# RMSNorm with swish on one core: the first 32 rows stored through GpSimd's queue, in two pieces

## The chip, the cores and the metric

The kernel runs on one core of a Trainium2 chip. The core has five engines with instruction streams of their own: TensorE (PE), VectorE (DVE), ScalarE (ACT), GpSimd (POOL) and SyncE (SP), and 16 DMA engines that move data between the chip's large memory (HBM) and the on-chip buffer (SBUF, 128 partitions). The metric is the device time of one execution in microseconds, as a median of several runs. Profiles come from one further execution; all stretches of time below are counted from the start of its span.

## The reference

```python
batch, seq, dim = 16, 1024, 512          # x: float32, gamma: ones(dim), eps: 1e-5

def reference(x, gamma, eps):
    rms = np.sqrt(np.mean(x ** 2, axis=-1, keepdims=True) + eps)
    x_norm = x / rms * gamma
    return (x_norm * (1.0 / (1.0 + np.exp(-x_norm)))).astype(np.float32)
```

There are 16384 rows of 512 float32 numbers: 33.55 MB in, and as much out.

## The kernel before

**Tiling.** Each of the 128 partitions gets 128 rows. They are numbered 0 to 127 here, and a "row" below means one row in every partition (128 x 2 KB = 256 KB). The rows are cut into groups of 32, 48, 16 and 32 (L28), within which a partition's rows lie side by side in HBM, so a DMA of n rows is one contiguous run of n x 2 KB for each partition. All rows live in one SBUF buffer, `xb`, which is a ring of 96 slots (L29): row a sits in slot a mod 96, is normalised and activated in place, and is stored from there. Rows 96 to 127 therefore reuse the slots of rows 0 to 31, and their loads have to wait until those rows have been stored.

**Transfers.** `loads` (L30) and `stores` (L32) list the DMAs as (first row, number of rows); "load 80" is the load that begins at row 80. All of them are issued by SyncE, in the order that `order` (L33 to L37) writes out by hand: the loads up to row 79 in one go; then, when load 64 has landed, the store of rows 0 to 31 and, right behind it, load 80, whose slots are free from the start; then, when that store has landed, loads 96, 112 and 126; then, when load 112 has landed, the remaining five stores. The loop at L153 to L169 turns the list into instructions: `load` is a DMA that adds 16 to its own semaphore when it has landed, "landed" and "stored" are waits of SyncE on such semaphores, and a store (L119) itself waits until `s_swish` says that enough units are finished. SyncE works through this list in order, so a wait holds back everything behind it.

**Computing.** The rows are worked through in 16 units of 8 rows (`cn`). For each unit ScalarE squares and sums six rows (L215), VectorE the other two (L251); GpSimd adds eps (`aeps`, L183) and raises to the power -1/2 (`rstd`, L189); VectorE multiplies each row by its factor and gamma (L260); ScalarE applies the swish in place (L225, L245) and counts `s_swish` up. The first unit is split four and four. TensorE computes nothing: for each unit it waits for the loads and for `s_eps` (L172 to L176) and then gives ScalarE its permit `s_land` for the squares. GpSimd's loop over the units k = 0 to 15 (L181 to L193) holds just the two operations, each behind a semaphore.

Of the kernel before, what the change touches and what calls it, by code (L numbers as in the profile page):

```python
# [9 lines left out]
def kernel(  # L10
# [7 lines left out]
    nc = tc.nc  # L18
# [6 lines left out]
    of = out.flatten_outer_dims()  # L25
# [3 lines left out]
    ring = 96  # L29
    loads = [(0, 4), (4, 4), (8, 8), (16, 8), (24, 8), (32, 16), (48, 16), (64, 11), (75, 5)]  # L30
    loads += [(80, 16), (96, 16), (112, 14), (126, 2)]
    stores = [(0, 32), (32, 32), (64, 16), (80, 16), (96, 24), (120, 8)]  # L32
    order = [("load", a) for a in (0, 4, 8)] + [("gamma", 0)]  # L33
    order += [("load", a) for a in (16, 24, 32, 48, 64, 75)]
    order += [("landed", 64), ("store", 0), ("load", 80)]
    order += [("stored", 0), ("load", 96), ("load", 112), ("load", 126)]
    order += [("landed", 112)] + [("store", a) for a in (32, 64, 80, 96, 120)]  # L37
    early = 2
    cn = 8
    own = 2  # L40
    own_first = 4
# [12 lines left out]
    load_at = {a: t for t, (a, _) in enumerate(loads)}  # L54
    store_at = {a: t for t, (a, _) in enumerate(stores)}
# [21 lines left out]
    junk_v = [sbuf(f"junk_v{j}", [P, D]) for j in range(own_first)]  # L77

    ld = [nc.alloc_semaphore(f"ld{t}") for t in range(len(loads))]
    st = [nc.alloc_semaphore(f"st{t}") for t in range(2)]  # L80
    s_gld = nc.alloc_semaphore("s_gld")
    s_zero = nc.alloc_semaphore("s_zero")
    s_half = nc.alloc_semaphore("s_half")
# [10 lines left out]
    def need(ins, sem, value):  # L94
        return ins.wait_op(sem, value, "sem-ge")
# [4 lines left out]
    def dram(ap, piece):  # L100
        a, n = piece
        g = max(g for g in range(len(groups)) if first[g] <= a)
        r = a - first[g]
        assert r + n <= groups[g], piece
        rows = ap[P * first[g] : P * (first[g] + groups[g])]
        return rows.rearrange("(p n) d -> p n d", n=groups[g])[:, r : r + n, :]

    def buf(piece):
        a, n = piece
        at = a % ring  # L110
        assert at + n <= ring, piece
        return xb[:, at : at + n, :]

    def load(t):
        return nc.sync.dma_start(
            out=buf(loads[t]), in_=dram(xf, loads[t])
        ).then_inc(ld[t], 16)

    def store(t):  # L119
        need(  # L120
            nc.sync.dma_start(out=dram(of, stores[t]), in_=buf(stores[t])),
            s_swish, ends[t],
        ).then_inc(st[min(t, 1)], 16)

    def check_order():
        issued, stored = [], set()
        for what, a in order:
            if what == "stored":
                stored.add(a)
            if what == "load":  # L130
                n = loads[load_at[a]][1]
                for c, m in stores:
                    if c + ring < a + n and a < c + m + ring:
                        assert c in stored, (a, c)
            issued.append((what, a))
        assert [a for what, a in issued if what == "load"] == list(load_at)
        assert [a for what, a in issued if what == "store"] == list(store_at)

    check_order()

    entry = nc.main_func.blocks[0].instructions
# [11 lines left out]
    for what, a in order[early:]:  # L153
        if what == "load":
            load(load_at[a])
        elif what == "store":
            store(store_at[a])
        elif what == "gamma":
            need(
                nc.sync.dma_start(  # L160
                    out=gamma4[0:P:32, :], in_=gamma.partition_broadcast(4)
                ),
                s_zero, 1,
            ).then_inc(s_gld, 16)
        elif what == "landed":
            nc.sync.wait_ge(ld[load_at[a]], 16)
        else:
            assert store_at[a] == 0
            nc.sync.wait_ge(st[0], 16)  # L169
    nc.sync.wait_ge(st[1], 16 * (len(stores) - 1))  # L170

    for k in range(1, K):  # L172
        for t, (a, n) in enumerate(loads):
# [5 lines left out]
    nc.gpsimd.memset(neg_half, -0.5).then_inc(s_half, 1)  # L179
    nc.gpsimd.wait_ge(s_half, 1)  # L180
    for k in range(K):  # L181
        need(
            nc.gpsimd.tensor_scalar(  # L183
                out=aeps[k % 2], in0=ms[min(k, 1)], scalar1=eps_f, scalar2=None, op0=ALU.add,
            ),
            s_sum, k + 1,
        ).then_inc(s_eps, 1)
        need(
            nc.gpsimd.tensor_tensor(  # L189
                out=rstd[:, k * cn : (k + 1) * cn], in0=aeps[k % 2], in1=neg_half, op=ALU.pow  # L190
            ),
            s_eps, k + 1,
        ).then_inc(s_rstd, 1)  # L193
# [92 lines left out]
    k = K - 1  # L286
# [39 lines left out]
```

## Time and profile before

| what | value |
|---|---|
| runs | median 159.60 us of 3 (159.54 to 159.78) |
| the profiled execution | 160.54 us, of which the span of the program's instructions is 159.2 us |
| busy: DVE, ACT, POOL | 107.7, 115.7, 42.9 us |
| moved by DMA | 67.12 MB in 2744 packets, one queue |
| store of rows 0 to 31 | issued 48.27, landed 71.14 |
| load 80 | issued 48.66, landed 80.90 |
| loads 96, 112, 126 | issued 71.16 to 72.44, landed 90.62, 99.40, 100.65 |
| the other five stores | issued from 99.47 to 136.84, the last landed at 159.15 |

How to read it: the profile counts an engine as busy while it computes; instructions that only wait or issue a DMA count as idle (they appear as SPq, ACTq and so on). A DMA's issue is a short instruction of the engine that issues it (0.33 to 0.49 us on SyncE here), while its data move later on the 16 DMA engines, and "landed" is the time at which its semaphore has its full count. The DMA lines of the page give, in 40 equal slices of the span, the busy share of the DMA engines in tenths and the GB/s, where a packet is counted whole in the slice in which it starts, so neighbouring slices can be over and under the true rate.

### The profile page before, as it was taken

What the parts mean: (1) busy time and instruction counts of PE and PEld (TensorE: products, weight loads), DVE (VectorE), ACT (ScalarE), POOL (GpSimd) and SP (SyncE); (2) the same over time, 40 slices, a digit from 0 to 9 for tenths busy, and PEclk for the clock granted to TensorE, in tenths of its full rate; (3) what the DMA queues carried; (4) which work ended last, traced back from release to release, by engine and by line L of the source; (5) the groups of instructions that cost most, each with busy time, mean ns of one, the idle gap of its engine ahead of it and who ended that gap; (6) DMA issues with size and microseconds to landing.
All of it is one profiled execution on the core that took longest, in us unless ns stands there. A gap on an engine that the chain in (4) does not pass through costs nothing. (4 is left out here: it accounts for less than half of the span.)

```text
span 159.2 us, 844 instructions
## 1 busy us (share of the span) xinstructions
DVE 107.7 (68%) x198; ACT 115.7 (73%) x205; POOL 42.9 (27%) x38
## 2 busy tenths in 40 slices
DVE  0051899798989989898916988989898993000000
ACT  3608389999999999999369999999999296200000
POOL 1040516061533516061502442606062400000000
DMA  7999999999899969969999998969969999999997
GB/s 261 447 418 445 424 494 412 395 453 469 362 422 534 527 263 527 511 272 395 436 469 412 428 396 364 532 263 527 527 263 403 519 395 395 531 457 395 395 395 329
DMA packets 2744, 67.12 MB, mean 422 GB/s; under 512 B 308, under 2 KB 308, under 8 KB 440
## 3 DMA queue, kind: packets, MB, share of 16 engines
q1 hardware_dynamic: 2744, 67.12, 98.6%
HBM read 33.56 MB, written 33.55 MB: 422 GB/s over the span
## 5 line engine op out<-in xcount | busy, mean ns | idle before, releaser
L260 DVE SCALAR_TENSOR_TENSOR xb<-xb,rstd,gamma_sb 128x512 f32 (+1 forms) x128 | 86.1, 745 | 0.0
L215 ACT ACTIVATE junk<-xb 128x512 f32 (+1 forms) x94 | 54.5, 580 | 13.2 <-ACTq L98 11.5
L225 ACT ACTIVATE xb<-xb x14 | 50.4, 3603 | 0.7 <-ACTq L98 0.7
L251 DVE SCALAR_TENSOR_TENSOR junk_v<-xb 128x512 f32 (+1 forms) x34 | 22.1, 689 | 23.1 <-DVEq L98 23.1
L189 POOL TENSOR_TENSOR rstd<-aeps,neg_half 128x8 f32<-128x8 f32 x16 | 31.7, 1984 | 1.3
L183 POOL TENSOR_SCALAR aeps<-ms 128x8 f32<-128x8 f32 x16 | 10.3, 647 | 79.2 <-DVE junk_v L251 79.2
L215 ACT ACTIVATION_READ_ACCUMULATOR junk<-xb 128x1 f32 x94 | 17.7, 188 | 0.0
L245 ACT ACTIVATE xb<-xb 128x4096 f32<-128x4096 f32 x2 | 7.2, 3616 | 5.0 <-DVE xb L260 5.0
L251 DVE DVE_READ_ACCUMULATOR junk_v<-xb 128x1 f32 x34 | 2.8, 82 | 0.0
L227 ACT ACT_TABLE_LOAD x1 | 1.3, 1283 | 1.9 <-PEq L62 1.9
L269 DVE LOAD_MASK_SELECT gamma_sb<-gamma x1 | 0.0, 14 | 2.0 <-DMA gamma<-in_gamma_dram 2.0
L178 POOL MEMSET gamma<- 128x512 f32 x1 | 0.5, 524 | 1.5 <-POOLq L62 1.5
L269 DVE STREAM_SHUFFLE gamma_sb<-gamma 128x512 f32<-128x512 f32 x1 | 0.7, 717 | 0.0
L307 POOL MEMSET const-float32-0.0<- 128x1 f32 x1 | 0.1, 98 | 0.2 <-issue 0.2
L179 POOL MEMSET neg_half<- 128x8 f32 x1 | 0.1, 104 | 0.0
L307 POOL MEMSET const-bfloat16-1.0<- 128x1 bf16 x1 | 0.1, 101 | 0.0
L307 POOL MEMSET const-uint8-127<- 128x1 uint8 x1 | 0.1, 101 | 0.0
L307 POOL MEMSET const-float32-1.0<- 128x1 f32 x1 | 0.1, 98 | 0.0
## 6 DMA issues: line engine op xcount, KB each, us to landing
xb<-in_x_dram SPq DMA_DIRECT2D x4, 4096.0 KB, 30.0
out_dram<-xb SPq DMA_DIRECT2D x2, 4096.0 KB, 30.1
xb<-in_x_dram SPq DMA_DIRECT2D x3, 2048.0 KB, 14.0
out_dram<-xb SPq DMA_DIRECT2D x1, 6144.0 KB, 23.1
xb<-in_x_dram SPq DMA_DIRECT2D x1, 3584.0 KB, 27.9
xb<-in_x_dram SPq DMA_DIRECT2D x1, 2816.0 KB, 43.1
xb<-in_x_dram SPq DMA_DIRECT2D x2, 1024.0 KB, 5.9
out_dram<-xb SPq DMA_DIRECT2D x1, 2048.0 KB, 22.6
```

Source lines behind the costliest of these rows:

```text
L178: nc.gpsimd.memset(gamma4, 0.0).then_inc(s_zero, 1)
L179: nc.gpsimd.memset(neg_half, -0.5).then_inc(s_half, 1)
L183: nc.gpsimd.tensor_scalar(out=aeps[k % 2], in0=ms[min(k, 1)], scalar1=eps_f, scalar2=None, op0=ALU.add,),
L189: nc.gpsimd.tensor_tensor(out=rstd[:, k * cn : (k + 1) * cn], in0=aeps[k % 2], in1=neg_half, op=ALU.pow),
L215: nc.scalar.activation(out=dummies[j], in_=rows[j], func=AF.Square, scale=inv_d**0.5, accum_out=sums[:, j : j + 1],)
L225: nc.scalar.activation(out=rows, in_=rows, func=AF.Silu).then_inc(s_swish, 1)
L227: nc.scalar.preload_act_table_set("silu_and_others")
L245: nc.scalar.activation(out=rows, in_=rows, func=AF.Silu), s_norm, n + 1
L251: ins = nc.vector.scalar_tensor_tensor(out=junk_v[j], in0=rows[j], scalar=inv_d, in1=rows[j], op0=ALU.mult, op1=ALU.mult, accum_out=to[:, ...
L260: ins = nc.vector.scalar_tensor_tensor(out=rows[j], in0=rows[j], scalar=factors[j], in1=gamma_sb, op0=ALU.mult, op1=ALU.mult,)
L269: need(nc.vector.stream_shuffle(gamma_sb, gamma4, [0] * 32), s_gld, 16).then_inc(s_gamma, 1)
L307: nc = _bacc.Bacc("TRN2", target_bir_lowering=False, num_devices=1)
```

## The change

The store of rows 0 to 31 is cut into one of 26 rows and one of 6. Both are issued by GpSimd, on its own DMA queue, inside its loop over the units: ahead of unit 6's two operations (`apart_at`) it waits for load 64 to have landed and issues both stores, each of which waits for four finished units as before. SyncE no longer issues that store. It issues load 80 when the 26 rows have landed, where before it did so right behind the store, and loads 96, 112 and 126 when the six rows have landed too. Each of the two stores has a semaphore of its own. All else is the same: the other stores, the loads and the operations of all engines.

```diff
-    stores = [(0, 32), (32, 32), (64, 16), (80, 16), (96, 24), (120, 8)]
+    stores = [(0, 26), (26, 6), (32, 32), (64, 16), (80, 16), (96, 24), (120, 8)]
     order = [("load", a) for a in (0, 4, 8)] + [("gamma", 0)]
     order += [("load", a) for a in (16, 24, 32, 48, 64, 75)]
-    order += [("landed", 64), ("store", 0), ("load", 80)]
-    order += [("stored", 0), ("load", 96), ("load", 112), ("load", 126)]
+    order += [("stored", 0), ("load", 80)]
+    order += [("stored", 26), ("load", 96), ("load", 112), ("load", 126)]
     order += [("landed", 112)] + [("store", a) for a in (32, 64, 80, 96, 120)]
     early = 2
+    apart = 2
+    apart_at = 6
...
-    st = [nc.alloc_semaphore(f"st{t}") for t in range(2)]
+    st = [nc.alloc_semaphore(f"st{t}") for t in range(apart + 1)]
...
-    def store(t):
+    def store(t, queue=nc.sync):
         need(
-            nc.sync.dma_start(out=dram(of, stores[t]), in_=buf(stores[t])),
+            queue.dma_start(out=dram(of, stores[t]), in_=buf(stores[t])),
             s_swish, ends[t],
-        ).then_inc(st[min(t, 1)], 16)
+        ).then_inc(st[min(t, apart)], 16)
...
         else:
-            assert store_at[a] == 0
-            nc.sync.wait_ge(st[0], 16)
-    nc.sync.wait_ge(st[1], 16 * (len(stores) - 1))
+            nc.sync.wait_ge(st[store_at[a]], 16)
+    nc.sync.wait_ge(st[apart], 16 * (len(stores) - apart))
...
     for k in range(K):
+        if k == apart_at:
+            nc.gpsimd.wait_ge(ld[load_at[64]], 16)
+            for t in range(apart):
+                store(t, nc.gpsimd)
         need(
             nc.gpsimd.tensor_scalar(
                 out=aeps[k % 2], in0=ms[min(k, 1)], scalar1=eps_f, scalar2=None, op0=ALU.add,
```

More of the change, by code (lines that the diff above doesn't have):

```diff
@@ L136, in check_order @@
         assert [a for what, a in issued if what == "load"] == list(load_at)
-        assert [a for what, a in issued if what == "store"] == list(store_at)
+        assert [a for what, a in issued if what == "store"] == list(store_at)[apart:]
     check_order()
```

## The prediction

> **What bounds the kernel now.** I read the page first, then the DMA queue's own waits, the timelines around 48 and 99 us, a table of short windows, and the trace's packet records (one record for each piece that one of the 16 DMA engines moves). From the page:
>
> ```profile
> span 159.2 us, 844 instructions
> ...
> DVE 107.7 (68%) x198; ACT 115.7 (73%) x205; POOL 42.9 (27%) x38
> ...
> DMA  7999999999899969969999998969969999999997
> ...
> q1 hardware_dynamic: 2744, 67.12, 98.6%
> HBM read 33.56 MB, written 33.55 MB: 422 GB/s over the span
> ```
>
> No engine is over 73% busy, while the one DMA queue fills 98.6% of 16 engines' span. Loads and stores run at the same pace: a 32768-byte packet (load) takes 1.215 us and a 65536-byte packet (store) 2.418 us, 27 GB/s an engine or 433 for 16. At that pace 67.12 MB take 155.0 us, so at most 4 us of the span are not pure transfer. The head takes about 2 of them (first packet at 1.00 us, slow ones until 1.9). The page's chain ends with computing at 136.5 us, and the last store lands at 159.15, so the chain says nothing of the end. What SyncE waits for:
>
> ```profile
> SPq L166 <- DMA xb<-in_x_dram: 69.1, 2, 42.1
> SPq L121 <- ACT xb L245: 25.9, 2, 20.9
> SPq L170 <- DMA out_dram<-xb: 22.3, 1, 22.3
> SPq L115 <- DMA out_dram<-xb: 22.1, 1, 22.1
> ```
>
> The fourth line is the wait for the 32-row store, 22.1 us long, and it costs nothing: load 80 is queued behind the store and keeps the DMA engines fed from 70.8 to 80.9, while the loads after it are issued at 71.16. So the stall that the change reshapes is already covered. The one hole is elsewhere:
>
> ```profile
> 98.00:99.00 1.00, 0.79 (x2) 1.00 (x3) 0.00 (x0) 1.00 0.96 393
> 99.00:100.00 1.00, 0.63 (x3) 1.00 (x3) 0.00 (x0) 1.00 0.16 62
> 100.00:101.00 1.00, 1.00 (x5) 1.00 (x1) 0.23 (x1) 1.00 2.50 1057
> ```
>
> These windows (the last two columns are the DMA share and GB/s, a packet counted whole where it starts) show the engines empty around 99.5. SyncE issues the next stores when load 112 has landed on all 16 engines (99.40, issue 99.47), their data start at 100.31, and only the two rows of load 126 cover this. By the packet records 15 engines had ended load 112 by 98.21, one at 99.10. That **one late engine** sets the restart, and with it the end. It lost its time in two packets: its last store packet at 67.17 took 3.64 us in place of 2.42 (five others lost 0.1 to 0.6 there), just before the first packets of load 80, and its last packet of load 112 took 1.40 in place of 1.06. Because it began 0.5 us ahead of the last engine, it passed that one by 0.7 at 70.8 (70.82 against the 70.12 that the last starter needed). So the quantity to forecast is when the slowest engine has moved everything up to load 112.
>
> **The change, part by part.**
>
> *The start of the store (A).* SyncE issued it at 48.27, with its data first at 50.23 to 50.80, as each engine ended load 75: the queue never ran dry. Now GpSimd issues it. Its rows:
>
> ```profile
> 46.29 0.68 POOL L183 TENSOR_SCALAR aeps<-ms 128x8 f32<-128x8 f32 x1 [4.42 <-DVE junk_v L251]
> 47.05 2.00 POOL L189 TENSOR_TENSOR rstd<-aeps,neg_half 128x8 f32<-128x8 f32 x1
> 53.47 0.67 POOL L183 TENSOR_SCALAR aeps<-ms 128x8 f32<-128x8 f32 x1 [4.42 <-DVE junk_v L251]
> ```
>
> Both new waits are over by then (load 64 at 48.17, the fourth swish at 48.24), so the issue starts when unit 5's power ends, at 49.05. From there to the first byte no row shows GpSimd. From below, SyncE's own 0.84 us (99.47 to 100.31) gives 49.9, before any engine is free, and costs nothing. From above, a GpSimd instruction can take the 2.0 of its power, and the first DMA of the program took 1.00 to its first packet: 52.05, which is 1.25 after the slowest engine's 50.80. I take SyncE's 0.84 plus two of GpSimd's small operations at 0.68 (both have to be worked through by GpSimd), a start near 51.1 and **+0.3 us**. An idle stretch here also puts all engines in step, so the spread of 0.57 us is gone and a late packet can't hide behind a head start any more. The Trainium skill, "DMA: Bandwidth & Descriptors", section "Latency and other measured facts", gives about 0.6 us to the first byte for SyncE's path and about 1 for GpSimd's; by that estimate the start would be near 50.3 and A nothing.
>
> Behind the two issues on GpSimd stands unit 6's aeps, due at 53.47. The gap is 4.42 us. TensorE passes aeps on as the permit for ScalarE's squares of unit 7 (at 55.33, with aeps done at 54.14), so 1.2 us more are free, and the 4.08 us that ScalarE waits for load 80 (77.0 to 81.06) take up the next 4. I cost it at nothing; it would show only if the issues held GpSimd for 9 us and more.
>
> *Load 80 behind the 26 rows.* 26 rows are eight packets of 53248 bytes an engine, 15.7 us by the 27 GB/s, so from 51.1 to 66.8; landing adds 0.33 (70.82 to 71.14 before) and SyncE 0.84, so load 80 starts near 68.0. The six rows (8 x 0.455 = 3.6 us) run until 70.4 by themselves and cover this with 2.4 us to spare: nothing.
>
> *Loads 96, 112, 126 behind the six rows.* At 68.0 some five of the eight small packets are left. Taking turns with load 80's packets of 1.215 us, they need 5 x 1.67 = 8.4 us, land near 76.7, and load 96 starts at 77.6, while load 80 lasts until 80.1: covered by 2.5 us. If load 80 went first instead, the store would end at 80.1, and 0.33 + 0.84 = 1.2 us would be lost. The same page, section "Queues, rings and completion order", says that an engine takes its queues in turn, packet by packet; no run here shows two queues at once, and by it the cover holds.
>
> *The change of direction (B).* Before, one passage from store to load cost the late engine 1.22 us, and 0.24 as a mean of 16. Now each engine passes some five times between small store packets and load packets. From below: the two are in different queues and the loss goes, -0.7 us on the slowest engine (or -1.0 with the 0.33 of its last packet). From above: a loss like that happens again at a second passage of the same engine, +1.2, and with the order above another 1.2. I take one loss on the slowest engine of 1.2 that the head start no longer hides (0.5 of it was hidden before): **+0.4 us**, nearest to the one row there is.
>
> *The rest.* SyncE issues take 0.33 to 0.49 us, and none was waited for; taking two issues off it saves nothing. The stores behind load 112 and the last 59 us are untouched; computing is ahead of them by 8 us (rows 96 to 119 issued at 131.21, data first at 139.20).
>
> **Sum:** +0.3 + 0.4 = +0.7 us. The profiled execution took 160.54 us (span 159.2 and 1.3 around it), so it would be 161.2; that execution is 0.94 over the median of the runs shown, 159.60, so the forecast for the median is **160.3 us**. Part of the 0.94 may be that late engine itself, which the other runs then didn't have; this speaks against a gain.
>
> **The rivals.**
>
> *The late engine recovers (faster, 0.29).* If the loss at 67 us comes of a load queued right behind a store in one queue, the change takes it away. With A at nothing to 0.3 the slowest engine gains 0.4 to 1.0 us: 158.9, range 158.6 to 159.25. For it: the loss stands at that passage and at none from store to store (the last packets at 117.45 and 138.13 take their usual time). Against it: the 0.94, and a start that leaves a hole. It decides for itself as soon as B is under -0.3 - A.
>
> *Nothing changes (0.16).* The bytes, the pace and the covers are the same, and A and B cancel or are nothing: 159.6, within 0.3. The page named above, section "Issuing engines are not separate DMA queues", says this of DMAs from several engines: they share the 16 DMA engines, and only issue time is saved. The rows agree in that no issue was waited for. The change's own promise would then be empty.
>
> *The software queue moves smaller pieces, or starts late (slower by more, 0.12).* Packets of 4096 bytes took 0.159 us and those of 2048 bytes 0.084, 5 and 11% over the pace. The 32 rows take 19.35 us, so +1.0 or +2.1, with A 161.0 to 162.0.
>
> *The forecast (0.43):* slower by 0.3 to 1.3 us, 159.9 to 160.9.
>
> **Numbers.** 0.2% of this time is 0.3 us, about what a measurement here can tell from no change. Faster 0.29, same 0.16, slower 0.43 + 0.12 = 0.55. The range takes in most of the faster rival and the slower one to its middle: 158.8 to 161.5, leaving out some 0.05 below and 0.08 above, beside what I have not thought of. As cases of both signs are likely, the forecast's own range stands above.
>
> **What would show it.** In the profile after: a second DMA queue with about 8.39 MB; its first packet (A right if 50.8 to 51.6; no cost if earlier); packet size 53248 and 12288 (smaller: the third rival); a start of load 80 near 68 with no empty engine before it; packets of both queues side by side until about 76; their length against 1.215 and 0.455 (B); the landing of load 112 against 99.40 and the first packet of the next stores against 100.31. If 112 lands before 99 the first rival is right. Wrong altogether would be: GpSimd held for many microseconds so that units come late after 81, or a hole between 70 and 82.

## The result, and the profile after

The changed kernel took 161.05 us (median of 5 runs, 160.42 to 161.36) against 159.60 for the kernel before: a ratio of 1.008, with an interval of 1.0061 to 1.0098. It is slower by 0.8%, inside the range of 158.8 to 161.5 and above the 160.3 that was forecast. The profiled execution took 161.36 us, with a span of 160.0. From its page:

```profile
span 160.0 us, 845 instructions
...
DVE 107.7 (67%) x198; ACT 115.7 (72%) x205; POOL 44.1 (28%) x40
...
DMA  7999999999999999999999998969969999999997
...
q1 hardware_dynamic: 2600, 58.73, 86.1%
q0 software_dynamic: 288, 8.39, 12.7%
```

The second queue is there with its 8.39 MB. Computing is the same to 0.1 us, except that GpSimd is busy 1.2 us longer, with the two issues. The DMA engines look as full as before, but the same bytes now need a longer span. Full and slow are told apart below.

GpSimd's part, from its timeline (start, length, instruction, idle time before it):

```profile
46.82 2.00 POOL L194 TENSOR_TENSOR rstd<-aeps,neg_half 128x8 f32<-128x8 f32 x1
48.78 1.31 POOL L123 DMA_DIRECT2D out_dram<-xb  x2
53.26 0.67 POOL L188 TENSOR_SCALAR aeps<-ms 128x8 f32<-128x8 f32 x1 [3.16 <-DVE junk_v L256]
```

Two issues take 1.31 us together, fit into the gap of 4.4, and delay nothing: aeps still waits 3.16 us for VectorE. By the packet records, the first 53248-byte packet starts at 50.13, as soon as the first engine has ended load 75; there is no hole.

The passage from the store to load 80, in a table of two windows (busy times of VectorE, ScalarE and GpSimd, clock, DMA share, GB/s):

```profile
66.50:68.50 2.00, 2.00 (x6) 2.00 (x1) 0.80 (x2) 1.00 0.98 412
68.70:70.50 1.80, 1.80 (x4) 1.80 (x4) 1.68 (x1) 1.00 0.91 218
```

A window counts a packet whole where it starts, so its last two columns can be off by the packets at its edges. With each packet's bytes spread evenly over its record, no engine is idle in either window, but they move 425 GB/s in the first and 265 in the second. By the records, the last two 12288-byte packets of each engine take 0.62 to 0.92 us in place of 0.46, on all 16 engines, from 68.8 on. The first packets of load 80 follow at 70.51, and five of them take 0.4 to 1.2 us too long. SyncE had issued the load at 66.83, when the 26 rows had landed. The six rows landed at 71.16.

ScalarE and the hole near 100 us, from its timeline (the kernel before first, then the changed one) and another table of windows:

```profile
81.06 0.60 ACT L215 ACTIVATE junk<-xb 128x512 f32 x1 [4.08 <-ACTq L98]
81.90 0.60 ACT L220 ACTIVATE junk<-xb 128x512 f32 x1 [5.16 <-ACTq L100]
```

```profile
99.00:100.00 1.00, 0.64 (x1) 1.00 (x5) 0.00 (x0) 1.00 0.80 328
100.00:101.00 1.00, 0.80 (x3) 1.00 (x2) 0.00 (x0) 1.00 0.28 115
101.00:102.00 1.00, 1.00 (x3) 1.00 (x1) 0.39 (x1) 1.00 2.48 1049
```

Load 80 comes 0.84 us later for ScalarE, and the hole that stood at 99 us stands 0.8 later: load 112 landed at 100.19 (99.40 before), the next stores' data start at 101.12 (100.31). All that follows is the same, 0.8 us later. The kernel before was profiled in an execution 0.94 us over its median, this one in one 0.31 over its own, so these 0.8 us understate the 1.45 between the medians.

### The profile page after: what moved, and what is told of

It reads as the page before. It is cut to its first block, busy times and chain, and to the rows that moved or that the text cites. A ratio compares the mean times of both kernels' runs of the same rounds, so it can differ in the third digit from the quotient of the medians.

```text
span 160.0 us, 845 instructions
## 1 busy us (share of the span) xinstructions
DVE 107.7 (67%) x198; ACT 115.7 (72%) x205; POOL 44.1 (28%) x40
## 3 DMA queue, kind: packets, MB, share of 16 engines
q0 software_dynamic: 288, 8.39, 12.7%
## 5 line engine op out<-in xcount | busy, mean ns | idle before, releaser
L220 ACT ACTIVATE junk<-xb 128x512 f32 (+1 forms) x94 | 54.6, 580 | 14.0 <-ACTq L100 12.7
L220 ACT ACTIVATION_READ_ACCUMULATOR junk<-xb 128x1 f32 x94 | 17.7, 189 | 0.0
L123 POOL DMA_DIRECT2D out_dram<-xb x2 | 1.3, 654 | 0.0
```

The source lines that it names most:

```text
L123: queue.dma_start(out=dram(of, stores[t]), in_=buf(stores[t])),
L220: nc.scalar.activation(out=dummies[j], in_=rows[j], func=AF.Square, scale=inv_d**0.5, accum_out=sums[:, j : j + 1],)
```

## The experiments

Each kernel was timed beside the kernel before on the same chip (medians 159.63, 159.68, 159.69 and, for the last one, 159.91). **Lost at the passage** is worked out from the packet records of one execution: the length of the stretch from 66 to 74.5 us (61 to 69.5 for the cut at 16 and 16), less its bytes at 433.5 GB/s, with the bytes of a packet spread evenly over its record. In none of these kernels is an engine idle there, so this is time lost in packets that take too long. It is a mean of 16 engines, while the time goes by the last of them. Two kernels further down do the same as the kernel before up to 96 us, and lost 0.23 and 0.10 (experiments 10 and 12); one that does the same as the change lost 1.01 (experiment 11). So differences of some 0.15 in this column say nothing, and the medians decide.

| kernel | queue of the first store | packets ahead of load 80 | lost at the passage | median us | ratio to before |
|---|---|---|---|---|---|
| before | SyncE | 65536 | 0.27 | 159.6 | 1 |
| 6 and 26 rows | SyncE | 53248 | 0.26 | 159.77 | 1.0003 (0.9987 to 1.0019) |
| 26 and 6 rows | SyncE | 12288 | 0.43 | 160.11 | 1.0028 (1.0019 to 1.0037) |
| the same, with the waits | SyncE | 12288 | 0.44 | 160.01 | 1.0020 (1.0012 to 1.0029) |
| the same, with the waits | ScalarE | 12288 | 0.47 | 160.17 | 1.0024 (1.0009 to 1.0040) |
| 32 rows, load 80 behind | GpSimd | 65536 | 0.76 | 160.53 | 1.0035 (1.0023 to 1.0047) |
| 16 and 16 rows | GpSimd | 32768 | 1.15 | 160.89 | 1.0071 (1.0054 to 1.0087) |
| 26 and 6 rows, load 80 behind | GpSimd | 12288 | 1.00 | 161.17 | 1.0088 (1.0061 to 1.0114) |
| the change | GpSimd | 12288 | 1.11 | 161.05 | 1.0080 (1.0061 to 1.0098) |

The edits are to the changed kernel, but for the two that say otherwise; the assertions of the kernel on its own list change with them and are not shown.

The theories at the outset: **P**, the two queues slow each other at the passage; **W**, it is the load that is issued late, onto busy engines; **S**, it is the small packets that the cut puts ahead of the load.

**1. The cut alone.** Both stores go through SyncE's queue, with load 80 right behind.

```diff
-    order += [("stored", 0), ("load", 80)]
+    order += [("landed", 64), ("store", 0), ("store", 26), ("load", 80), ("stored", 0)]
...
-        if k == apart_at:
-            nc.gpsimd.wait_ge(ld[load_at[64]], 16)
-            for t in range(apart):
-                store(t, nc.gpsimd)
```

> The cut into 26 and 6 rows alone: both stores go through SyncE's queue, load 80 right behind them as in the kernel before. Theory P (two queues in the DMA engines at the same time slow the passage from store to load): 159.6 us, within 0.3 of the kernel before. Theory W (it is the load's late issue, onto engines busy with a store, whatever the queue): also 159.6. Rival S (small packets of 12288 bytes ahead of the load are what slows the passage): 160.5 to 161.1, as in the changed kernel.

160.11 us, between all expectations: the cut costs 0.45 us by itself, a third of the change. In the records the last store packets take up to 0.80 in place of 0.46, on about the last one or two packets of each engine. S has a share.

**2. The cut and the waits, in one queue.**

```diff
-    order += [("stored", 0), ("load", 80)]
+    order += [("landed", 64), ("store", 0), ("store", 26), ("stored", 0), ("load", 80)]
...
-        if k == apart_at:
-            nc.gpsimd.wait_ge(ld[load_at[64]], 16)
-            for t in range(apart):
-                store(t, nc.gpsimd)
```

> The cut and the waits, without the second queue: both stores through SyncE's queue, load 80 issued when the 26 rows have landed, the later loads when the 6 rows have. Theory P: 159.6, within 0.3, with store packets at 0.46 us to the end. Theory W: 160.5 to 161.1, with the last store packets stretched from about 2 us after load 80's issue. If it comes out between, both have a share.

160.01 us: no more than the cut alone, so W falls; issuing load 80 at 66.8 in place of 48.9 costs nothing. The same two windows as in the changed kernel:

```profile
66.50:68.50 2.00, 2.00 (x6) 2.00 (x1) 0.87 (x2) 1.00 1.02 436
68.70:70.50 1.80, 1.80 (x4) 1.80 (x4) 1.60 (x1) 1.00 1.30 482
```

With the packets spread evenly, the second window moves 364 GB/s here and 265 in the changed kernel, which differs in the queue alone. What is left of the change, 1.0 us, goes with GpSimd's queue.

**3. The second queue without the wait ahead of load 80.**

```diff
-    order += [("stored", 0), ("load", 80)]
+    order += [("landed", 64), ("load", 80), ("stored", 0)]
```

> The second queue without the wait ahead of load 80: GpSimd stores 26 and 6 rows, SyncE issues load 80 right after load 64 has landed, so both queues hold packets from 50 us on. Theory P, if the cost goes with the time that both queues are full: about half of a 19 us stretch is mixed in place of some 2 us, so 163 us or more, with stretched packets all through. Theory P, if the cost falls once, at the first meeting of the two: 160.5 to 161.5. Theory W: 159.6, since no load is issued late. If the engines take turns without loss, load 80 lands near 70 and the 32 rows near 80, the loads behind come a little late (about 1 us).

163.0 us, as P's dearer form had it, but for another reason. Three windows of this kernel:

```profile
50.20:54.40 4.20, 3.63 (x8) 4.20 (x7) 1.05 (x2) 1.00 1.17 387
56.00:76.00 20.00, 18.30 (x35) 20.00 (x37) 6.49 (x7) 1.00 1.00 434
80.90:82.90 2.00, 2.00 (x6) 2.00 (x1) 0.83 (x2) 1.00 0.02 6
```

The records don't name the engine; a packet is put down to the engine whose last one ended where it begins. So read, each engine takes its two queues in turn (53248 bytes out, 32768 in) from some 55 us until load 80's packets run out, at 71 to 74 us. Over these 16 to 19 us the pace is the full 433 GB/s, as it is in the window, whose last 2 to 5 us hold stores alone: running side by side costs nothing. What costs is the start of it (1.19 us lost from 49.5 to 57), and then the hole: sharing the engines, the stores end at 81 us, and only then the loads behind them may start. That hole and the slow first packets after it lose 3.2 us (78 to 87, of which 2.6 idle).

**4. No overlap at all.**

```diff
-    order += [("stored", 0), ("load", 80)]
-    order += [("stored", 26), ("load", 96), ("load", 112), ("load", 126)]
+    order += [("stored", 0)]
+    order += [("stored", 26), ("load", 80), ("load", 96), ("load", 112), ("load", 126)]
```

> The second queue without any overlap: GpSimd stores 26 and 6 rows, and load 80 and the later loads are issued when both have landed. A hole of 0.3 (landing) and 0.8 (issue to data), 1.2 us in all, stands between store and load. Theory P: no packet is stretched, so the hole alone is paid: 159.6 + 1.2 = 160.8, about 0.2 under the changed kernel, and the engines start in step. Theory W: the same. A third, H (the first loads after a long stretch of stores are slow whatever the queue): 1.2 and 1.0 more, 161.8.

162.22 us, over all expectations and nearest to H. Two windows:

```profile
69.60:71.50 1.90, 1.90 (x4) 1.90 (x7) 0.81 (x1) 1.00 0.00 0
71.50:73.50 2.00, 1.43 (x4) 2.00 (x7) 0.00 (x0) 1.00 1.06 311
```

The hole is 1.9 us as a mean of the engines, not 1.2: the landing takes 0.45 (70.03 to 70.48), and from the issue at 70.56 to the data 1.0 us pass on the first engine and 1.9 on the last. Then the first packet of load 80 takes 1.4 to 2.2 us in place of 1.21 on every engine, 0.67 too long as a mean. The store packets before it keep their 0.46 to the end. So after stores and a hole it is the load's first packets that take longer. That the stretched store packets of the other kernels are the same cost, moved ahead because the load is already queued, is a guess that no run here tests.

**5. ScalarE's queue in place of GpSimd's.** ScalarE's loop over the units (its squares are L220 of the profile after) becomes a function `units(a, b)` and is run in two parts, so that ScalarE can issue the stores between them:

```diff
...
+    units(0, 4)
+    nc.scalar.wait_ge(ld[load_at[64]], 16)
+    for t in range(apart):
+        store(t, nc.scalar)
+    units(4, K - 2)
...
-        if k == apart_at:
-            nc.gpsimd.wait_ge(ld[load_at[64]], 16)
-            for t in range(apart):
-                store(t, nc.gpsimd)
```

> The changed kernel with GpSimd's queue exchanged for ScalarE's: ScalarE's loop over the units is cut in two, and between them it waits for load 64 and issues the 26 and the 6 rows; SyncE waits as in the changed kernel. So far one queue with the same cut and the same waits gave 160.0, GpSimd's queue 161.05. Theory Q2 (a second queue of whatever kind costs about 1 us where its store meets the load): 161.0, with last store packets near 0.9 us. Theory G (it is GpSimd's queue in particular): 160.0, with last store packets near 0.7 as in the one-queue kernel. The cut of the loop and two issues on ScalarE cost some 2 us of computing at 48 us, which the wait for load 80 takes up.

160.17 us, as theory G had it. The same two windows as in the changed kernel:

```profile
66.50:68.50 2.00, 1.43 (x5) 2.00 (x5) 0.00 (x0) 1.00 1.05 449
68.70:70.50 1.80, 1.80 (x5) 1.80 (x1) 1.17 (x2) 1.00 1.23 439
```

439 GB/s stand where GpSimd's queue had 218. Much of that gap is the counting: first packets of load 80 begin inside the window here and count whole, while in the changed kernel none begins before 70.51. With the packets spread evenly it is 362 against 265. A second queue as such costs nothing that these runs can tell from one queue with the same cut.

**6. The cut the other way round, in one queue.**

```diff
-    stores = [(0, 26), (26, 6), (32, 32), (64, 16), (80, 16), (96, 24), (120, 8)]
+    stores = [(0, 6), (6, 26), (32, 32), (64, 16), (80, 16), (96, 24), (120, 8)]
...
-    order += [("stored", 0), ("load", 80)]
-    order += [("stored", 26), ("load", 96), ("load", 112), ("load", 126)]
+    order += [("landed", 64), ("store", 0), ("store", 6), ("load", 80), ("stored", 0)]
+    order += [("stored", 6), ("load", 96), ("load", 112), ("load", 126)]
...
-        if k == apart_at:
-            nc.gpsimd.wait_ge(ld[load_at[64]], 16)
-            for t in range(apart):
-                store(t, nc.gpsimd)
```

> One queue, no wait ahead of load 80, the cut the other way round: 6 rows first, then 26, so that the packets ahead of load 80 are large (53248 bytes). 26 and 6 with the small ones last gave 160.11 against 159.63. Theory S (the small packets ahead of the load expose it): 159.6 to 159.75. Rival C (a second store, its 128 more packets and its semaphore, cost the 0.45 wherever it stands): 160.1.

159.77 us, no difference from the kernel before: it is not the second store that costs but the size of the packets ahead of the load. S is right for its share, the 0.45.

**7. GpSimd's queue with large packets.**

```diff
-    stores = [(0, 26), (26, 6), (32, 32), (64, 16), (80, 16), (96, 24), (120, 8)]
+    stores = [(0, 16), (16, 16), (32, 32), (64, 16), (80, 16), (96, 24), (120, 8)]
...
-    order += [("stored", 26), ("load", 96), ("load", 112), ("load", 126)]
+    order += [("stored", 16), ("load", 96), ("load", 112), ("load", 126)]
```

> The changed kernel with the cut at 16 and 16 rows, so load 80 is issued when 16 rows have landed (near 60 us) and meets packets of 32768 bytes in GpSimd's queue for some 10 us and more. Theory M (each time a load of SyncE's queue and a store of GpSimd's start to run side by side, about 1 us is lost, whatever the packets): 160.7 to 161.2, as in the changed kernel. Theory S alone (only small packets ahead of the load are stretched): 159.6 to 159.9. If the two run side by side without loss afterwards, the pace is 433 GB/s from 64 us on.

160.89 us, as theory M had it. Large packets don't cure it. Between 63.6 and 67.7 us the 32768-byte packets take up to 2.42 in place of 1.21; from 68 on both queues run side by side at 433 GB/s. The loss falls once, some 3 us after the load's issue at 60.74.

**8. One queue again, but GpSimd's.** Load 80 is issued by GpSimd too, right behind the 6 rows (`load` gets a queue as `store` has).

```diff
-    order += [("stored", 0), ("load", 80)]
+    order += [("stored", 0)]
...
             for t in range(apart):
                 store(t, nc.gpsimd)
+            load(load_at[80], nc.gpsimd)
```

> GpSimd issues the 26 rows, the 6 rows and, right behind them, load 80 too, so the passage from store to load lies inside GpSimd's queue; SyncE waits for the 6 rows and issues loads 96, 112 and 126. Theory M (the loss comes of GpSimd's queue and SyncE's meeting): the passage costs what the cut costs, 160.1; the meeting of load 80 with load 96 is load with load and costs nothing. Rival G1 (GpSimd's queue passes from store to load slowly by itself): 160.7 to 161.2.

161.17 us: M falls, G1 holds. The passage loses 1.00 us although no other queue takes part in it. P and M, "the two queues meet", were the wrong picture; GpSimd's queue is enough. This kernel differs from that of the first experiment in the queue alone: 1.0088 against 1.0028 of the kernel before, so with these small packets the queue costs about 1.0 us.

**9. The cleanest comparison: the kernel before, with two DMAs on GpSimd's queue.** No cut, no wait ahead of load 80; SyncE waits for the store and then issues loads 96, 112 and 126.

```diff
-    stores = [(0, 26), (26, 6), (32, 32), (64, 16), (80, 16), (96, 24), (120, 8)]
+    stores = [(0, 32), (32, 32), (64, 16), (80, 16), (96, 24), (120, 8)]
...
-    order += [("stored", 0), ("load", 80)]
-    order += [("stored", 26), ("load", 96), ("load", 112), ("load", 126)]
+    order += [("stored", 0)]
+    order += [("load", 96), ("load", 112), ("load", 126)]
...
-    apart = 2
+    apart = 1
...
             for t in range(apart):
                 store(t, nc.gpsimd)
+            load(load_at[80], nc.gpsimd)
```

> The kernel before with nothing changed but the queue of two DMAs: GpSimd issues the store of 32 rows, uncut, and load 80 right behind it; SyncE waits for the store and issues loads 96, 112 and 126. No cut, no wait ahead of load 80, large packets (65536 bytes), one queue across the passage. Theory G1 (a store of GpSimd's queue loses about 1 us where a load follows, by its queue alone, against 0.25 in SyncE's): 160.4 to 160.8. Rival (GpSimd's queue costs only together with small packets or with a second queue): 159.6 to 159.8.

160.53 us against 159.91 of the kernel before on the same chip, a ratio of 1.0035 (1.0023 to 1.0047): some 0.6 us for the queue alone. That is the way of G1, but less than it said: its 160.4 would be 0.8 over a kernel before at 159.6. One window, of the kernel before first and then of this one:

```profile
67.00:70.40 3.40, 3.40 (x9) 3.40 (x4) 2.48 (x2) 1.00 1.12 453
67.00:70.40 3.40, 3.40 (x9) 3.40 (x4) 2.42 (x2) 1.00 0.98 337
```

With the packets spread evenly these are 403 and 355 GB/s. The last 65536-byte packet of every engine takes 2.67 to 3.50 us in place of 2.42; in the kernel before five engines had such a packet (2.94 to 3.64) and the other eleven took 2.42 to 2.51. The passage accounts for 0.49 of the 0.6 us (0.76 lost in place of 0.27). The start gives another 0.1: GpSimd issues the store at 49.07 in place of 48.27, and 0.18 us are lost from 48 to 54 us in place of 0.06.

**10 to 12. The wait for load 112.** The prediction had named the hole behind this wait as the place through which a late engine sets the end. Three kernels leave the wait out, so that the stores stand right behind the last load; the third also has the last 16 rows as one load:

```diff
-    order += [("landed", 112)] + [("store", a) for a in (32, 64, 80, 96, 120)]
+    order += [("store", a) for a in (32, 64, 80, 96, 120)]
```

The kernel before without the wait:

> The kernel before without SyncE's wait for load 112: the last five stores stand right behind load 126 and wait for finished units alone. Theory E (the slowest engine's end of load 112, its landing and the issue make the hole at 99 us, and through it set the end): no hole, 0.5 to 1.0 us faster, 158.6 to 159.1, and a late engine no longer delays the others. Rival: stores queued that early meet the loads in the DMA engines and cost as much as they save, 159.6 or slower.

160.50 us, a ratio of 1.0048 (1.0029 to 1.0067): slower, as the rival had it. The hole is gone and nothing is won, since the packets of load 126 are stretched:

```profile
98.00:99.00 1.00, 0.43 (x2) 1.00 (x3) 0.00 (x0) 1.00 0.86 115
```

The 4096-byte packets take up to 1.04 us in place of 0.16, and 1.09 us are lost from 96 to 102.

The changed kernel without the wait:

> The changed kernel without SyncE's wait for load 112. Theory E: the loss at 69 to 73 us (about 1.06 us as a mean of 16 engines) stays, but the hole at 100 goes: 160.0 to 160.4, that is 0.6 to 1.0 under the changed kernel; the distance to the kernel before without that wait is the loss at the passage by itself, 1.0 to 1.4. Rival: the hole only takes up what the passage left uneven, and nothing is gained: 161.0.

160.98 us, a ratio of 1.0077 (1.0050 to 1.0105) to the kernel before, no different from the changed kernel with the wait.

The kernel before without the wait, with one load for the last 16 rows:

```diff
-    loads += [(80, 16), (96, 16), (112, 14), (126, 2)]
+    loads += [(80, 16), (96, 16), (112, 16)]
...
-    order += [("stored", 0), ("load", 96), ("load", 112), ("load", 126)]
+    order += [("stored", 0), ("load", 96), ("load", 112)]
```

> The kernel before without the wait for load 112 and with its last 16 rows as one load, so that packets of 32768 bytes, not of 4096, stand ahead of the stores. Without the wait but with the 2-row load it took 160.5, its 4096-byte packets stretched from 0.16 to 0.3 and up to 1.0 us. Theory S (small packets ahead of a change of direction are what is stretched; large ones hide it): no hole and no stretch, 158.5 to 159.0, faster than both kernels. Rival (any load with stores queued behind it loses about 1 us at 98 us): 160.3 or more.

159.74 us, a ratio of 1.0014 (0.9996 to 1.0033): no difference, so it doesn't beat the kernel before. With 32768-byte packets the stretch from 96 to 102 us loses 0.49 in place of 1.09. With the wait and its hole, the kernel of the sixth experiment lost 0.65 there. S holds for the size, and its forecast of no loss was too good: a passage from load to store, with the stores long in the queue, isn't free either.

## Why the prediction was right, and where not

- **The number.** 161.05 lies in the range of 158.8 to 161.5, but that took in cases of both signs, so this says little; it lies above the forecast's own 159.9 to 160.9. The direction was right, and the place; the size was not: +1.45 came where +0.7 was forecast. The steps below say which terms were off.
- **What bounds the kernel** was read rightly: the DMA engines. Computing was the same and nothing of the time moved with it.
- **A, the start of the store, +0.3:** mis-sized. GpSimd's first issue stands at 48.78 and the data start at 50.13, before the last engines are free. There was no hole. Only the first packet of seven engines is 0.1 to 0.2 too long: from 48 to 54 us the stretch lost 0.19 in place of 0.06. A was about +0.1.
- **GpSimd's following operations and the issues themselves:** right. 1.31 us in a gap of 4.4.
- **The covers of load 80 and of loads 96 to 126:** right in the sum (no engine idle from 66 to 96), wrong in the picture. The queues didn't take turns at the passage: all small packets went first, load 80's followed at 70.51, and the six rows landed at 71.16, not near 76.7. The Trainium skill, "DMA: Bandwidth & Descriptors", section "Queues, rings and completion order", says that an engine takes its queues in turn by packets. The third experiment agrees, with turns from 55 us until the load's packets ran out at 71 to 74; at this passage no such turn shows.
- **B, the change of direction, +0.4:** the right place and sign, and the mis-sized term. It lost 1.11 us as a mean of the engines in place of 0.27, +0.84. The step took "one loss like the one before" on one engine as the nearest row (its own figures, 1.2 of which 0.5 had been hidden, would give +0.5); what came was a loss on all 16. Two things made it larger, each shown apart: packets of 12288 bytes ahead of the load (+0.4 to 0.5 us in the median, experiments 1, 2 and 6), and GpSimd's queue (about 0.6 with large packets, experiment 9; about 1.0 on top of the cut, experiments 1 and 8).
- **From the profile to the median:** the whole 0.94 us by which the profiled execution of before exceeded its median was taken off, though the prediction itself suspected that part of it was the late engine. The records bear the suspicion out. The sixth experiment's kernel has the median of the kernel before within 0.1 us, and its profiled execution (159.81) has no late engine: there load 112 ends between 97.65 and 98.27, and the next stores' data start at 99.56. In the profile of before they start at 100.31, 0.75 later, which is most of the 0.94. In the changed kernel they start at 101.12, 1.55 after 99.56, and that is the whole difference between the two executions (161.36 and 159.81). So the change cost 0.82 profile against profile, near the +0.7 that was summed, and 1.45 median against median. That nearness is partly luck: the last engine ended load 112 only 0.75 later (99.85 against 99.10) because the profile of before had a late one, while the mean of the engines ended it 1.09 later (99.08 against 97.99).
- **The rivals.** "The late engine recovers" fell: a separate queue didn't take the loss away but enlarged it, and the ninth experiment shows it with nothing else changed. "Nothing changes" fell with the interval. "Smaller pieces", whose 161.0 to 162.0 holds the measured time, fell too: the packets are 53248 and 12288 bytes, at 1.971 and 0.468 us, within 2% of SyncE's queue (1.966 and 0.460).
- **One queue or several.** The prediction had weighed the section "Issuing engines are not separate DMA queues" of the Trainium skill, "DMA: Bandwidth & Descriptors". For ScalarE's queue the runs agree (160.17 against 160.01 in one queue). For GpSimd's they don't: what it says would give no change, and the measurement is +0.35% with two DMAs moved to that queue and nothing else changed.

**Left open.** Why a store of GpSimd's queue is stretched on all engines where a load follows is not settled; the records show that it is so, not what the engine waits for. It isn't the issue: in the changed kernel GpSimd's two issues had ended at 50.09, almost 19 us before the first stretched packet. It goes with the store's queue and not with the load's, since the loss is as large with load 80 in GpSimd's queue (1.00) as in SyncE's (1.11); a load alone moved to GpSimd's queue was not tried. In one queue of SyncE's or ScalarE's small packets are stretched too, but less (0.43 to 0.47). The two costs are not independent: 0.45 for the cut and 1.0 for the queue on top of it make up the 1.45, while the queue with large packets costs 0.6.

## What to carry to other kernels

Where the DMA engines are the bound, a busy share near 1 doesn't say that they move at their pace: look at the length of packets of the same size where stores and loads change over, above all at the last packets ahead of the change. By these runs, let large packets stand there, and try SyncE's or ScalarE's queue before GpSimd's for a store that a load follows; a wait that is covered by queued transfers has nothing to give, however long it is. And when a profiled execution lies well above the median of its kernel, find out what it has that the others may not have before a gain is counted from it.

## What the runs showed of the hardware that was not expected

- A store of GpSimd's queue with a load behind it lost 0.76 to 1.15 us at the passage, one of SyncE's or ScalarE's 0.10 to 0.47 (the kernel before, experiments 1, 2, 5 to 10 and 12).
- Loads and stores of two queues shared the engines for 16 to 19 us at 433 GB/s, the pace of either alone; only the start of the sharing cost, about 1.2 us (experiments 3 and 7).
- After a stretch of pure stores and a hole, the first packet of a load of 32768 bytes took 1.4 to 2.2 us in place of 1.21, on each of the 16 engines (experiment 4).
- Packets of 4096 bytes with stores queued behind them took up to 1.04 us in place of 0.16 (experiment 10).
- GpSimd's two issues of 128 pieces each took 0.65 us, against 0.33 to 0.49 for an issue of SyncE's, and ran beside VectorE's work without delaying it.
